# Binary cross-entropy on one core: runs of 8320 columns in place of 8192, the last four chunks 6272

## The chip, the cores and the metric

The kernel runs on one core of a Trainium2 chip, whose other cores are idle. The metric is device time in microseconds (us). Repeated runs of the kernel before spread over 1868.3 to 1873.6 us, so a difference under about 0.15% is not seen here.

## The reference

```python
def setup_inputs():
    return {
        "pred": np.random.uniform(0.01, 0.99, (8192, 8192)).astype(np.float32),
        "target": np.random.randint(0, 2, (8192, 8192)).astype(np.float32),
    }

def reference(pred, target):
    eps = 1e-7
    pred = np.clip(pred, eps, 1 - eps)
    return -(target * np.log(pred) + (1 - target) * np.log(1 - pred))
```

Two arrays of 268 MB are read and one is written. As target is 0 or 1, the kernel computes -ln|target - 1 + pred|.

## The kernel before

The arrays are taken as flat memory and cut into 64 chunks. A chunk is 128 rows of 8192 columns, one row for each of the 128 partitions of SBUF, the memory on the chip that the engines compute on. It lies in one piece in HBM, the large memory that holds the arrays, so the pitch (the distance from one partition's row to the next) is 32 KiB. Two rings of four slots in SBUF hold pred (fp32, computed on in place) and target (cast to bf16 by the load). In the profile's lines, DVE is VectorE and ACT is ScalarE, which compute, POOL is GpSimd, which issues most of the transfers, and SP (SPq) is SyncE, which issues the rest.

```python
W = 8192
SLOTS = 4
    # ...
    def chunks(ap):
        return ap.rearrange("r c -> (r c)").rearrange("(k p w) -> k p w", p=P, w=W)
    # ...
    def load(k):
        queue = nc.sync if k == 0 else nc.gpsimd
        queue.dma_start(out=slot(ring_p, k), in_=pred_c[k])
        nc.gpsimd.dma_start(out=slot(ring_t, k), in_=target_c[k])
    # ... store: as load, on nc.sync for the last two chunks
    # clip: one VectorE instruction on ring_p
    # front: VectorE (t - 1) + p, then ScalarE Abs and Ln; back: VectorE * -1
        for k in range(1, n - 1):
            clip(k)
            front(k)
            back(k - 1)
            store(k - 1)
            if k >= 2 and k - 2 + SLOTS < n:
                load(k - 2 + SLOTS)
    # ... the last chunk in four quarters of compute, stored in two halves
```

## Time and profile before

| | before |
|---|---|
| time, median of 3 runs | 1870.49 us |
| span of the profiled run | 1867.5 us |
| VectorE, ScalarE, POOL busy | 60%, 48%, 6% |
| HBM over the span | 431 GB/s |
| packets | 27,797 |

The page's slices cut the span in forty; a digit is the busy share in tenths. "Packets" are the single moves that the 16 DMA engines make. A load or a store of a chunk is 128 data packets of one row each; the 3088 packets under 512 B are 16 more for each of the 193 transfers, 4 B each in the records, and are called its completion writes here.

### The profile page before, as it was taken

What the parts mean: (1) busy time and instruction counts of PE and PEld (TensorE: products, weight loads), DVE (VectorE), ACT (ScalarE), POOL (GpSimd) and SP (SyncE); (2) the same over time, 40 slices, a digit from 0 to 9 for tenths busy, and PEclk for the clock granted to TensorE, in tenths of its full rate; (3) what the DMA queues carried; (4) which work ended last, traced back from release to release, by engine and by line L of the source; (5) the groups of instructions that cost most, each with busy time, mean ns of one, the idle gap of its engine ahead of it and who ended that gap; (6) DMA issues with size and microseconds to landing.
All of it is one profiled execution on the core that took longest, in us unless ns stands there. A gap on an engine that the chain in (4) does not pass through costs nothing.

```text
span 1867.5 us, 759 instructions
## 1 busy us (share of the span) xinstructions
DVE 1117.6 (60%) x199; ACT 902.4 (48%) x136; POOL 110.6 (6%) x193
## 2 busy tenths in 40 slices
DVE  4846564656656656566565665656656566566664
ACT  3643635546355364553644535445354463544635
POOL 0210000000000000000000000000000000000000
DMA  9999999999999999999999999999999999999999
GB/s 326 337 378 350 352 376 344 377 352 351 381 345 374 358 344 386 343 371 362 344 388 341 366 368 344 386 344 360 370 344 384 348 355 375 345 378 355 348 381 344
DMA packets 27797, 671.14 MB, mean 359 GB/s; under 512 B 3088, under 2 KB 3088, under 8 KB 3088
## 3 DMA queue, kind: packets, MB, share of 16 engines
q0 software_dynamic: 27216, 658.52, 98.9%
q1 hardware_dynamic: 576, 12.58, 1.6%
q14 instruction: 5, 0.04, 0.0%
HBM read 536.87 MB, written 268.44 MB: 431 GB/s over the span
## 4 chain that ended last, share of the span: by engine, by line
issue 87%; DMA 6%; POOL 5%; DVE 1%; ACT 1%; POOLq 0%; DVEq 0%; PEldq 0%
DMA ring_t<-in_target_dram 4%; DMA out_dram<-ring_p 2%; POOL ring_t L59 2%; POOL out_dram L63 2%; POOL ring_p L58 1%; DVE ring_p L73 1%; ACT ring_p L77 0%; ACT ring_p L76 0%; DVE ring_p L81 0%; POOLq L58 0%; DVEq L73 0%; PEldq L138 0%; POOLq L63 0%
## 5 line engine op out<-in xcount | busy, mean ns | idle before, releaser
L76 ACT ACTIVATE ring_p<-ring_p 128x8192 f32<-128x8192 f32 (+1 forms) x67 | 450.6, 6725 | 949.5 <-DVE ring_p L73 949.5
L73 DVE SCALAR_TENSOR_TENSOR ring_p<-ring_t,ring_p 128x8192 f32<-128x8192 bf16 (+1 forms) x67 | 556.6, 8309 | 326.0 <-DMA ring_t<-in_target_dram 326.0
L67 DVE TENSOR_SCALAR ring_p<-ring_p 128x8192 f32<-128x8192 f32 x64 | 283.3, 4426 | 406.6 <-DMA ring_p<-in_pred_dram 406.6
L77 ACT ACTIVATE ring_p<-ring_p 128x8192 f32<-128x8192 f32 (+1 forms) x67 | 450.6, 6725 | 2.1
L81 DVE TENSOR_SCALAR ring_p<-ring_p 128x8192 f32<-128x8192 f32 (+1 forms) x67 | 283.3, 4228 | 5.0 <-ACT ring_p L77 5.0
L63 POOL DMA_DIRECT2D out_dram<-ring_p x62 | 40.8, 659 | 1691.8 <-DVE ring_p L81 1661.8
L58 POOL DMA_DIRECT2D ring_p<-in_pred_dram x63 | 36.1, 574 | 18.7 <-DMA out_dram<-ring_p 18.4
L59 POOL DMA_DIRECT2D ring_t<-in_target_dram x64 | 35.3, 552 | 0.8 <-PEq L138 0.8
L87 ACT ACT_TABLE_LOAD x1 | 1.3, 1283 | 0.7 <-PEq L127 0.7
L86 DVE MEMSET warm<- 1x8 f32 x1 | 0.1, 65 | 0.8 <-PEq L127 0.8
L87 ACT ACTIVATE warm<-warm 1x8 f32<-1x8 f32 x1 | 0.2, 208 | 0.0
L127 POOL MEMSET const-float32-0.0<- 128x1 f32 x1 | 0.1, 98 | 0.2 <-issue 0.2
L127 POOL MEMSET const-bfloat16-1.0<- 128x1 bf16 x1 | 0.1, 101 | 0.0
L127 POOL MEMSET const-float32-1.0<- 128x1 f32 x1 | 0.1, 98 | 0.0
L127 POOL MEMSET const-uint8-127<- 128x1 uint8 x1 | 0.1, 98 | 0.0
## 6 DMA issues: line engine op xcount, KB each, us to landing
ring_p<-in_pred_dram POOLq DMA_DIRECT2D x63, 4096.0 KB, 34.5
out_dram<-ring_p POOLq DMA_DIRECT2D x62, 4096.0 KB, 25.3
ring_t<-in_target_dram POOLq DMA_DIRECT2D x64, 2048.0 KB, 43.7
ring_p<-in_pred_dram SPq DMA_DIRECT2D x1, 4096.0 KB, 19.5
out_dram<-ring_p SPq DMA_DIRECT2D x1, 4096.0 KB, 20.2
out_dram<-ring_p SPq DMA_DIRECT2D x2, 2048.0 KB, 11.6
```

Of the source, the lines that this page charges most:

```text
L58: queue.dma_start(out=slot(ring_p, k), in_=pred_c[k])
L59: nc.gpsimd.dma_start(out=slot(ring_t, k), in_=target_c[k])
L63: queue.dma_start(out=out_c[k, :, off : off + w], in_=slot(ring_p, k, off, w))
L67: nc.vector.tensor_scalar(out=p, in0=p, scalar1=EPS, scalar2=1 - EPS, op0=Alu.max, op1=Alu.min)
L73: nc.vector.scalar_tensor_tensor(out=p, in0=t, scalar=1.0, in1=p, op0=Alu.subtract, op1=Alu.add)
L76: nc.scalar.activation(out=p, in_=p, func=Act.Abs)
L77: nc.scalar.activation(out=p, in_=p, func=Act.Ln)
L81: nc.vector.tensor_scalar(out=p, in0=p, scalar1=-1.0, scalar2=None, op0=Alu.mult)
L86: nc.vector.memset(warm, 1.0)
L87: nc.scalar.activation(out=warm, in_=warm, func=Act.Ln)
L127: nc = _bacc.Bacc("TRN2", target_bir_lowering=False, num_devices=1)
```

## The change

The intent: at 8192 fp32 columns the partitions' rows start a power of two (32 KiB) apart. 8320 columns make it 33,280 B. Four narrower chunks take up the remainder and shorten the work after the last load.

```diff
-W = 8192
+UNIT = 128
+WIDE, LAST = 65 * UNIT, 49 * UNIT
 SLOTS = 4
+def plan(total):
+    n = (total - 4 * LAST) // WIDE
+    widths = [WIDE] * n + [LAST] * 4
+    assert sum(widths) == total
+    return widths
 ...
-    def chunks(ap):
-        return ap.rearrange("r c -> (r c)").rearrange("(k p w) -> k p w", p=P, w=W)
+    def chunk(ap, k):
+        flat = ap.rearrange("r c -> (r c)")
+        return flat[cols[k] * P : (cols[k] + widths[k]) * P].rearrange("(p w) -> p w", p=P)
 ...
-    ring_p = pool.tile([P, SLOTS * W], fp32, name="ring_p", tag="ring_p")
-    ring_t = pool.tile([P, SLOTS * W], bf16, name="ring_t", tag="ring_t")
+    ring_p = pool.tile([P, SLOTS * WIDE], fp32, name="ring_p", tag="ring_p")
+    ring_t = pool.tile([P, SLOTS * WIDE], bf16, name="ring_t", tag="ring_t")
 ...
-        q = W // 4
+        q = widths[n - 1] // 4
```

The rest of the diff gives each chunk its own width in load, store and compute.

More of the change, by code (lines that the diff above doesn't have):

```diff
@@ L38, with slot @@
     R, C = pred.shape
-    n = R * C // (P * W)
-    assert n * P * W == R * C and n > SLOTS
-    def chunks(ap):
-        return ap.rearrange("r c -> (r c)").rearrange("(k p w) -> k p w", p=P, w=W)
-    pred_c, target_c, out_c = chunks(pred), chunks(target), chunks(out)
+    widths = plan(R * C // P)
+    n = len(widths)
+    cols = [sum(widths[:k]) for k in range(n)]
+    def chunk(ap, k):
+        flat = ap.rearrange("r c -> (r c)")
+        return flat[cols[k] * P : (cols[k] + widths[k]) * P].rearrange("(p w) -> p w", p=P)
     pool = ctx.enter_context(tc.tile_pool(name="rings", bufs=1))
-    ring_p = pool.tile([P, SLOTS * W], fp32, name="ring_p", tag="ring_p")
-    ring_t = pool.tile([P, SLOTS * W], bf16, name="ring_t", tag="ring_t")
+    ring_p = pool.tile([P, SLOTS * WIDE], fp32, name="ring_p", tag="ring_p")
+    ring_t = pool.tile([P, SLOTS * WIDE], bf16, name="ring_t", tag="ring_t")
     warm = pool.tile([1, 8], fp32, name="warm", tag="warm")
-    def slot(ring, k, off=0, w=W):
-        c = k % SLOTS * W + off
+    def slot(ring, k, off=0, w=None):
+        w = w or widths[k]
+        c = k % SLOTS * WIDE + off
         return ring[:, c : c + w]
@@ L57, in load, with store, clip @@
         queue = nc.sync if k == 0 else nc.gpsimd
-        queue.dma_start(out=slot(ring_p, k), in_=pred_c[k])
-        nc.gpsimd.dma_start(out=slot(ring_t, k), in_=target_c[k])
-    def store(k, off=0, w=W):
+        queue.dma_start(out=slot(ring_p, k), in_=chunk(pred, k))
+        nc.gpsimd.dma_start(out=slot(ring_t, k), in_=chunk(target, k))
+    def store(k, off=0, w=None):
+        w = w or widths[k]
         queue = nc.sync if k >= n - 2 else nc.gpsimd
-        queue.dma_start(out=out_c[k, :, off : off + w], in_=slot(ring_p, k, off, w))
-    def clip(k, off=0, w=W):
+        queue.dma_start(out=chunk(out, k)[:, off : off + w], in_=slot(ring_p, k, off, w))
+    def clip(k, off=0, w=None):
         p = slot(ring_p, k, off, w)
@@ L69, in clip, with front @@
         )
-    def front(k, off=0, w=W):
+    def front(k, off=0, w=None):
         p, t = slot(ring_p, k, off, w), slot(ring_t, k, off, w)
@@ L77, in front, with back @@
         nc.scalar.activation(out=p, in_=p, func=Act.Ln)
-    def back(k, off=0, w=W):
+    def back(k, off=0, w=None):
         p = slot(ring_p, k, off, w)
```

## The prediction

> **What bounds the kernel now.** I read the page's span, its busy line and the slices first, then the DMA part, then the waits, then the timeline of a few chunks in the middle and of the end.
>
> ```profile
> span 1867.5 us, 759 instructions
> DVE 1117.6 (60%) x199; ACT 902.4 (48%) x136; POOL 110.6 (6%) x193
> ...
> DMA  9999999999999999999999999999999999999999
> ...
> DMA packets 27797, 671.14 MB, mean 359 GB/s; under 512 B 3088, under 2 KB 3088, under 8 KB 3088
> ...
> q0 software_dynamic: 27216, 658.52, 98.9%
> ...
> HBM read 536.87 MB, written 268.44 MB: 431 GB/s over the span
> ```
>
> No compute engine is over 60% busy, and the DMA engines are at nine tenths or more in all forty slices, the first and the last included. The 359 GB/s counts the bytes that a packet writes; a load of target reads fp32 and writes bf16, so it is counted at half. What the engines take in is the HBM line: 536.87 + 268.44 = 805.31 MB, 431 GB/s over the whole span. The kernel is one long stream of transfers with compute beside it.
>
> ```profile
> DVE ring_p L67 <- DMA ring_p<-in_pred_dram: 406.6, 61, 19.4
> DVE ring_p L73 <- DMA ring_t<-in_target_dram: 326.0, 63, 6.1
> ```
>
> In the waits (total us, times, longest) VectorE waits for loads 732.6 us in all; ScalarE waits for VectorE and is not what ends anything. The timeline of one chunk in the middle (start, us, engine and line) gives the period:
>
> ```profile
> 921.19 0.54 POOL L63 DMA_DIRECT2D out_dram<-ring_p  x1 [27.48 <-DVE ring_p L81]
> 921.72 0.54 POOL L58 DMA_DIRECT2D ring_p<-in_pred_dram  x1
> 922.24 0.55 POOL L59 DMA_DIRECT2D ring_t<-in_target_dram  x1
> ...
> 927.17 4.43 DVE L67 TENSOR_SCALAR ring_p<-ring_p 128x8192 f32<-128x8192 f32 x1 [6.27 <-DMA ring_p<-in_pred_dram]
> 936.93 8.69 DVE L73 SCALAR_TENSOR_TENSOR ring_p<-ring_t,ring_p 128x8192 f32<-128x8192 bf16 x1 [5.34 <-DMA ring_t<-in_target_dram]
> 945.54 4.42 DVE L81 TENSOR_SCALAR ring_p<-ring_p 128x8192 f32<-128x8192 f32 x1
> ```
>
> And the end:
>
> ```profile
> 1821.59 0.54 POOL L63 DMA_DIRECT2D out_dram<-ring_p  x1 [27.45 <-DVE ring_p L81]
> ...
> 1837.34 6.69 DVE L73 SCALAR_TENSOR_TENSOR ring_p<-ring_t,ring_p 128x2048 f32<-128x2048 bf16 x3 [0.97 <-DMA ring_t<-in_target_dram]
> ...
> 1854.77 1.23 DVE L81 TENSOR_SCALAR ring_p<-ring_p 128x2048 f32<-128x2048 f32 x1 [2.52 <-ACT ring_p L77]
> 1856.03 0.33 SPq L63 DMA_DIRECT2D out_dram<-ring_p  x1
> ```
>
> From the store issued at 921.19 to that at 1821.59 there are 31 chunks: 900.40 / 31 = 29.05 us a chunk. A chunk takes in 3 x 128 x 32,768 B = 12.58 MB: 433 GB/s. When POOL issues at 921.19, the loads queued before it still run until 927.17 and 936.93, so there are 15.7 us of work in the queue at each issue: the engines never run dry. The chain of waits calls 87% of the span "issue", because it follows POOL, which idles until its next turn; it names no cost.
>
> **What the Trainium skill says.** First, "DMA: Bandwidth & Descriptors", section "Where 436 GB/s comes from": 16 ports x 32 B x 850 MHz = 435.2 GB/s, 27.2 B/ns per engine. The trace agrees closely: the 433 GB/s of the steady chunks is 99.5% of it, and the trace's single packet records show 1213 ns as the median of a 32,768 B packet and 611 ns of the 16,384 B halves of the last store. The difference, 602 ns for 16,384 B, is 27.2 B/ns, which leaves about 9 ns fixed per packet. Consecutive packets overlap a little. Second, same page, section "Latency and other measured facts", the row on HBM row pitch at large powers of two: it measured 207 of 214 GB/s at a per-partition pitch of 512 KiB and half rate at 4 MiB, and nothing smaller. Here the pitch is 32 KiB and the packet medians stand at the port's rate, so this trace shows no such loss to recover. Third, same page, section "How a descriptor splits into AXI transactions": starts off a 256 B boundary cost beats. 33,280 B = 130 x 256, 25,088 = 98 x 256 and the half row of the last store 12,544 = 49 x 256, so all rows stay aligned; the trace of before can't show the unaligned case. Fourth, "SBUF — State Buffer", section "SBUF size: 192, 224, or 256?": about 208 KiB of a partition is usable. The rings grow from 4 x 8192 x 6 = 196,608 B to 4 x 8320 x 6 = 199,680 B, 195 KiB, and fit; no run shows the limit.
>
> **The change part by part.** The plan is 60 chunks of 8320 columns and four of 6272: 499,200 + 25,088 = 524,288 columns, 64 chunks as before. So nothing is removed or added: the same 759 instructions, the same 193 transfers of 128 rows, the same bytes, the same order and waits. Only sizes move.
>
> Transfers. One chunk is 24 packets per engine (3 x 128 / 16): 29.05 us / 24 = 1210.4 ns a packet, where the port's rate alone asks 32,768 / 27.2 = 1204.7. So 5.7 ns a packet are fixed, as an average with the overlap and the completion writes in it. A wide row: 33,280 / 27.2 + 5.7 = 1229.2 ns, x 24 = 29.50 us. A narrow row: 25,088 / 27.2 + 5.7 = 928.1 ns, x 24 = 22.27 us. Sum: 60 x 29.50 + 4 x 22.27 = 1770.0 + 89.1 = 1859.1 us against 64 x 29.05 = 1859.2. No change, and it doesn't matter whether the excess goes by packet or by byte.
>
> Compute, all beside the transfers. Wide: VectorE (4.43 + 8.69 + 4.42) x 65/64 = 17.8 us and ScalarE 2 x 7.03 x 65/64 = 14.3 us of a 29.50 us chunk. Narrow: x 49/64, 13.4 and 10.8 us of 22.27. The queue's reserve at each issue goes from 15.7 to 15.9 us, and to 12.0 us in the narrow chunks. The engines stay fed.
>
> The end. Before, the last load is waited for at 1837.34 and three stores, 12.58 MB or 29.05 us of transfer, are still to be moved; that puts the end of data near 1866. The last half store is issued 18.7 us after that load; its own data takes 29.05 / 6 = 4.8 us, so it had to be there by 29.05 - 4.8 = 24.2: 5.5 us of reserve. After, the stores left are 22.27 us, the last half 3.7 us, the deadline 18.6, and the chain of quarters shrinks to 18.7 x 49/64 = 14.3: 4.3 us of reserve. The end is bound by transfers in both, so the shorter last chunk buys nothing: the bytes that it no longer moves were moved earlier, at the same rate. What the narrow chunks do is leave the compute chain shorter beneath a queue that is shorter too.
>
> Start: the queue is filled by four loads at once and the first store comes long before they are done. A wider first chunk delays VectorE by about 0.3 us and the transfers by nothing.
>
> Sum: 1870.49 - 0.1, call it 1870.
>
> **The rivals.** (a) The pitch of 32 KiB does cost something and the new one frees it. For it speaks only the intent; against it, 99.5% of the port's rate. Were all 5.7 ns a packet to vanish, 64 x 24 x 5.7 ns = 8.8 us, giving 1862, 0.5% faster. A gain over 2% would need 37 us, four times that, and a rate of 440 GB/s, above the 435.2. (b) Rows over 32,768 B are cut into two packets. The largest packet in this trace is exactly 32,768 B, so it can't say. Then 60 x 24 = 1440 more packets per engine at 5.7 ns are +8.2 us, 1879; at 13 ns (the casting loads' packets have a larger fixed part: median 1227 ns for 32 KiB read) +19 us, 1889. Still about 1%. (c) The end is a compute chain after all, and shrinks: 4.4 us of quarters and 1.1 us of last store, 1865. The reserve of 5.5 us and the full last slice speak against it. (d) The new pitch hits the memory worse, or the engines drift apart more. Nothing speaks for it but that it is untried; to lose 2% each wide packet must take 26 ns more.
>
> **Range and chances.** Point 1870 us. The low end 1865 takes rival (c) or half of (a); the high end 1880 takes the mild form of (b). Faster by over 2% is shut out by the port's rate as the packets show it: 1%. Slower by over 2% needs (d) or a heavy form of (b): 3%. Within 2%: 96%.
>
> **What would show it.** In the profile of the changed kernel: 27,797 packets again (about 50,800 if wide rows are cut); stores of wide chunks issued 29.5 us apart and of narrow ones 22.3; the DMA row full to the last slice; HBM near 431 GB/s over the span; VectorE's three instructions at about 4.5, 8.83 and 4.5 us; a last issue some 14 us after the last load. Wrong would be: a wide period under 29.4 us (the pitch mattered), one over 29.6 (cut or slower packets), or DMA slices at the end below 9 (the narrow chunks let the queue run dry).

## The result

| | before | after |
|---|---|---|
| median of 4 runs | 1870.47 us | 1870.09 us |
| lowest to highest | 1869.30 to 1870.98 | 1869.18 to 1870.61 |
| span of the profiled run | 1867.5 us | 1867.3 us |
| packets | 27,797 | 27,797 |

The ratio is 0.9998, with a 95% interval of 0.9981 to 1.0016: the same.

From the page of the changed kernel:

```profile
span 1867.3 us, 767 instructions
DVE 1117.6 (60%) x199; ACT 902.3 (48%) x136; POOL 110.7 (6%) x193
...
DMA  9999999999999999999999999999999999999999
...
DMA packets 27797, 671.14 MB, mean 359 GB/s; under 512 B 3088, under 2 KB 3088, under 8 KB 3088
...
HBM read 536.87 MB, written 268.44 MB: 431 GB/s over the span
```

All that says what the time is made of is unchanged: DMA full in all forty slices, the same number of packets (so the rows over 32,768 B were not cut), 431 GB/s. The waits of VectorE (total us, times, longest):

```profile
DVE ring_p L78 <- DMA ring_p<-in_pred_dram: 410.1, 61, 20.0
DVE ring_p L84 <- DMA ring_t<-in_target_dram: 326.0, 63, 6.0
```

736.1 us in place of 732.6. The timeline in the middle, at the end of the wide chunks and at the last load and store (start, us, engine, line):

```profile
935.07 0.54 POOL L74 DMA_DIRECT2D out_dram<-ring_p  x1 [27.93 <-DVE ring_p L92]
...
951.07 8.83 DVE L84 SCALAR_TENSOR_TENSOR ring_p<-ring_t,ring_p 128x8320 f32<-128x8320 bf16 x1 [5.42 <-DMA ring_t<-in_target_dram]
959.81 4.49 DVE L92 TENSOR_SCALAR ring_p<-ring_p 128x8320 f32<-128x8320 f32 x1
...
1761.13 0.54 POOL L74 DMA_DIRECT2D out_dram<-ring_p  x1 [27.89 <-DVE ring_p L92]
1783.69 0.54 POOL L74 DMA_DIRECT2D out_dram<-ring_p  x1 [20.96 <-DVE ring_p L92]
1807.33 0.54 POOL L74 DMA_DIRECT2D out_dram<-ring_p  x1 [22.05 <-DVE ring_p L92]
1831.98 0.54 POOL L74 DMA_DIRECT2D out_dram<-ring_p  x1 [23.05 <-DVE ring_p L92]
...
1843.91 5.20 DVE L84 SCALAR_TENSOR_TENSOR ring_p<-ring_t,ring_p 128x1568 f32<-128x1568 bf16 x3 [0.70 <-DMA ring_t<-in_target_dram]
...
1858.65 0.33 SPq L74 DMA_DIRECT2D out_dram<-ring_p  x1
```

From 935.07 to 1761.13 are 28 wide chunks, 29.50 us each, where before it was 29.05; 65/64 of 29.05 is 29.50. The period grew by the bytes and by nothing else. The last three issues are 22.56, 23.64 and 24.65 us apart; that is taken up below.

The end, by stretches, before and then after (window, length, VectorE, ScalarE and POOL busy with counts, clock, DMA share, GB/s):

```profile
1855.00:1857.50 2.50, 1.00 (x1) 0.00 (x0) 0.00 (x0) 1.00 1.02 439
1857.50:1860.00 2.50, 0.00 (x0) 0.00 (x0) 0.00 (x0) 1.00 1.03 439
1860.00:1862.50 2.50, 0.00 (x0) 0.00 (x0) 0.00 (x0) 1.00 0.98 419
1862.50:1865.00 2.50, 0.00 (x0) 0.00 (x0) 0.00 (x0) 1.00 0.25 105
```

```profile
1855.00:1857.50 2.50, 0.69 (x1) 2.47 (x2) 0.00 (x0) 1.00 1.04 447
1857.50:1860.00 2.50, 0.98 (x1) 0.12 (x1) 0.00 (x0) 1.00 0.77 326
1860.00:1862.50 2.50, 0.00 (x0) 0.00 (x0) 0.00 (x0) 1.00 1.02 432
1862.50:1865.00 2.50, 0.00 (x0) 0.00 (x0) 0.00 (x0) 1.00 0.44 186
```

The share can exceed 1, as consecutive packets overlap. After, there is a dip to 0.77, about 0.25 x 2.5 = 0.6 us of missing transfer. The trace's packet records, counted by how many are in progress at a time, show what it is: at 1859.0 us six of the 16 engines have a packet and ten have none, while the last half store, issued at 1858.65, is still to come; from 1859.75 all 16 are busy. The kernel before has all 16 busy up to 1862.25. At 1863.0 there are still 16 busy after the change and 8 before it, but the last packet ends at 1865.8 us after and at 1866.0 before, and the span did not move.

### The profile page after: what moved, and what is told of

The parts are those of the page before. It is cut to its first block, busy times and chain, and to the rows that moved or that the text cites. A ratio compares the mean times of both kernels' runs of the same rounds, so it can differ in the third digit from the quotient of the medians.

```text
span 1867.3 us, 767 instructions
## 1 busy us (share of the span) xinstructions
DVE 1117.6 (60%) x199; ACT 902.3 (48%) x136; POOL 110.7 (6%) x193
## 2 busy tenths in 40 slices
DMA packets 27797, 671.14 MB, mean 359 GB/s; under 512 B 3088, under 2 KB 3088, under 8 KB 3088
## 4 chain that ended last, share of the span: by engine, by line
issue 88%; DMA 5%; POOL 5%; DVE 1%; ACT 1%; POOLq 0%; DVEq 0%; PEldq 0%
DMA ring_t<-in_target_dram 3%; DMA out_dram<-ring_p 2%; POOL ring_t L69 2%; POOL out_dram L74 2%; POOL ring_p L68 1%; DVE ring_p L84 1%; ACT ring_p L88 0%; ACT ring_p L87 0%; DVE ring_p L92 0%; POOLq L68 0%; DVEq L84 0%; PEldq L149 0%; POOLq L74 0%
## 5 line engine op out<-in xcount | busy, mean ns | idle before, releaser
L87 ACT ACTIVATE ring_p<-ring_p 128x8320 f32<-128x8320 f32 (+2 forms) x67 | 450.5, 6724 | 952.4 <-DVE ring_p L84 952.4
L84 DVE SCALAR_TENSOR_TENSOR ring_p<-ring_t,ring_p 128x8320 f32<-128x8320 bf16 (+2 forms) x67 | 556.6, 8310 | 326.1 <-DMA ring_t<-in_target_dram 326.0
L78 DVE TENSOR_SCALAR ring_p<-ring_p 128x8320 f32<-128x8320 f32 (+1 forms) x64 | 283.3, 4427 | 410.1 <-DMA ring_p<-in_pred_dram 410.1
L88 ACT ACTIVATE ring_p<-ring_p 128x8320 f32<-128x8320 f32 (+2 forms) x67 | 450.6, 6725 | 2.1
L92 DVE TENSOR_SCALAR ring_p<-ring_p 128x8320 f32<-128x8320 f32 (+2 forms) x67 | 283.3, 4229 | 4.0 <-ACT ring_p L88 4.0
```

What stands on the lines that cost most here:

```text
L78: nc.vector.tensor_scalar(out=p, in0=p, scalar1=EPS, scalar2=1 - EPS, op0=Alu.max, op1=Alu.min)
L84: nc.vector.scalar_tensor_tensor(out=p, in0=t, scalar=1.0, in1=p, op0=Alu.subtract, op1=Alu.add)
L87: nc.scalar.activation(out=p, in_=p, func=Act.Abs)
L88: nc.scalar.activation(out=p, in_=p, func=Act.Ln)
L92: nc.vector.tensor_scalar(out=p, in0=p, scalar1=-1.0, scalar2=None, op0=Alu.mult)
```

## The experiments

Two theories stood after the result. **One:** the kernel is a stream of transfers at the port's rate plus a few ns fixed per packet, the old pitch cost nothing, and the narrow end has nothing to shorten. **Two:** the pitch and the end each do something, and the two cancel. Twelve kernels were run on these and on what the pitch, the packet and compute cost. ("The port's rate" is the name that the prediction gives to 27.2 B/ns an engine. The packets show this rate; whether the port or something else sets it, no run separates.) In each, "before" is the kernel before on the same chip in the same rounds.

### The narrow end alone

```diff
-WIDE, LAST = 65 * UNIT, 49 * UNIT     # of the changed kernel
+WIDE, LAST = 64 * UNIT, 48 * UNIT     # 61 chunks of 8192, four of 6144
```

> The narrow end alone: 61 chunks of 8192 columns (pitch of 32 KiB kept) and four of 6144, 65 in all. Theory one, the stream of transfers is bound by the port's rate and a fixed few ns a packet: 61 x 29.05 + 4 x 24 x (24,576 / 27.2 + 5.7 ns) = 1772.1 + 87.3 = 1859.4 us of transfer against 1859.2, so 1870.6 us. Theory two, two effects cancelled in the change (the narrow end gains what the new pitch loses, or the reverse): 1866 or less, or 1874 or more.

Measured: 1869.59 us against 1870.09, ratio 0.9998 (0.9983 to 1.0013). As theory one has it. Its trace has the dip at the end too (seven engines with a packet at 1859.5 us).

### The wide runs alone

```diff
-WIDE, LAST = 65 * UNIT, 49 * UNIT     # of the changed kernel
+WIDE, LAST = 65 * UNIT, 8384
-    n = (total - 4 * LAST) // WIDE
-    widths = [WIDE] * n + [LAST] * 4
+    n = (total - 2 * LAST) // WIDE
+    widths = [WIDE] * n + [LAST] * 2  # 61 of 8320, two of 8384; slots of 8384
```

> The pitch alone, with no narrow end: 61 chunks of 8320 columns and two of 8384, 63 in all, no pitch a power of two. Theory one (port's rate): 61 x 29.50 + 2 x 24 x (33,536 / 27.2 + 5.7 ns) = 1799.5 + 59.5 = 1859.0, so 1870.3 us. Theory two (cancelling): the opposite sign of the run with the narrow end alone, 1874 or more or 1866 or less.

Measured: 1869.40 us against 1870.09, ratio 0.9995 (0.9980 to 1.0010). Its trace has no dip (all 16 engines busy up to 1862.0 us), so the dip is the narrow end's. Each part alone does nothing to the time; theory two falls. Neither half hides a gain or loss larger than 0.2%.

### Is the pitch ever a cost? 2 MiB, and a large pitch that is no power of two

```diff
-    .rearrange("(k p w) -> k p w", p=P, w=W)      # of the kernel before
+    .rearrange("(p k w) -> k p w", p=P, w=W)      # pitch 2 MiB
```

> The pitch made worse on purpose: each partition owns 524,288 columns in a row, so chunks of 8192 columns lie at a pitch of 2 MiB, a large power of two, with packets of the same 32 KiB. If the port's rate binds whatever the pitch: 1870 us. If the Trainium skill's row on large powers of two (164 of 214 GB/s at 2 MiB) carries over: packets of about 1.58 us and a period of 37.9 us, 64 x 37.9 + 11 = 2440 us.

Measured: 2059.31 us (2051.43 to 2066.52) against 1870.09, ratio 1.101 (1.0977 to 1.1043), result correct. So a power-of-two pitch can cost a great deal in this kernel, though a third of what the quoted row would have made of it. The page of this run:

```profile
span 2049.6 us, 759 instructions
...
DMA  9999999999999999999999999999999999999998
...
DMA packets 27797, 671.14 MB, mean 327 GB/s; under 512 B 3088, under 2 KB 3088, under 8 KB 3088
...
HBM read 536.87 MB, written 268.44 MB: 393 GB/s over the span
```

The engines are as "busy" as before, and move less: a full DMA row is no proof of full speed, and the HBM line (393 against 431 GB/s) must be read beside it.

The counterpart: a pitch nearly as large, 1,996,800 B.

```diff
-        return flat[cols[k] * P : (cols[k] + widths[k]) * P].rearrange("(p w) -> p w", p=P)
+        first = 0 if widths[k] == WIDE else n - 4      # of the changed kernel
+        wide = sum(x for x in widths if x == widths[k])
+        block = flat[cols[first] * P : (cols[first] + wide) * P].rearrange("(p w) -> p w", p=P)
+        c = cols[k] - cols[first]
+        return block[:, c : c + widths[k]]
```

> A large pitch that is no power of two: the 60 chunks of 8320 columns lie side by side in one block of pitch 1,996,800 B, the four of 6272 in one of 100,352 B. If only powers of two alias: 1870 us, and well below the run at 2 MiB if that is slow. If any pitch of megabytes costs: as slow as that run, 2400 us or so. If the port binds both: 1870 in both.

Measured: 1869.98 us, ratio 0.9999 (0.9982 to 1.0015). Megabytes of pitch cost nothing by themselves; 2 MiB does. (This run has the chunk widths of the changed kernel, the one at 2 MiB those of the kernel before; the widths alone make no difference, as the result shows.)

### Where the loss begins: 128 KiB, 512 KiB, 1 MiB

The edit is the same in all three, with g = 4, 16 or 32 chunks side by side:

```diff
-    .rearrange("(k p w) -> k p w", p=P, w=W)
+    .rearrange("(j p g w) -> j g p w", p=P, g=4, w=W)
-    in_=pred_c[k]               # target_c and out_c alike
+    in_=pred_c[k // 4, k % 4]
```

> The kernel before with four chunks side by side, so a pitch of 128 KiB, chunks of 8192 columns as before. If the loss seen at 2 MiB is one of very large powers of two: 1870 us. If it sets in just above 32 KiB, so that the kernel before stood at its edge: 1890 or more.

> The same with sixteen chunks side by side, a pitch of 512 KiB. The Trainium skill's row has 207 of 214 GB/s here; scaled by what 2 MiB lost in this case against that row (10% of the time against 30%), about 1%: 1890 us. No loss: 1870. The loss of 2 MiB already: 2050.

> The same with thirty-two chunks side by side, a pitch of 1 MiB, which the skill's row leaves out. Between the run at 512 KiB and that at 2 MiB: about 1960 us if the loss grows evenly; 1870 if it begins at 2 MiB.

| pitch | median us | ratio to before (95%) | packets of 32,768 B in the trace, 90th and 99th percentile, ns |
|---|---|---|---|
| 32 KiB (before) | 1870.49 | | 1213, 1226 |
| 128 KiB | 1870.08 | 0.9994 (0.9979 to 1.0009) | 1213, 1226 |
| 512 KiB | 1876.15 | 1.0027 (1.0011 to 1.0044) | 1213, 1258 |
| 1 MiB | 1910.13 | 1.0206 (1.0181 to 1.0231) | 1226, 1915 |
| 2 MiB | 2059.31 | 1.1010 (1.0977 to 1.1043) | 1580, 2419 |

Each ratio is to the kernel before in the same rounds (median 1870.36 us; 1870.09 for 2 MiB), not to the first row. The percentiles are of the POOL queue's packets; the median is 1213 ns in every row. The expectation at 512 KiB (1890) and that at 1 MiB (1960) were both too high: the loss grows steeply with each doubling rather than evenly. At 32 KiB the slow packets aren't there, and the kernel before does not stand at an edge: two doublings further there is still no loss. What makes a few packets slow no run shows.

### The fixed cost of a packet

```diff
-        queue.dma_start(out=slot(ring_p, k), in_=pred_c[k])
+        h = W // 4
+        for o in range(0, W, h):
+            queue.dma_start(out=slot(ring_p, k, o, h), in_=pred_c[k, :, o : o + h])
 # target's load and the store alike
```

> The kernel before with every transfer cut into column quarters, so four packets of 8 KiB a row in place of one of 32 KiB; bytes, chunks and waits of compute unchanged. Fixed cost by packet: 64 x 72 more packets an engine at 5.7 ns = +26 us, 1897; at the 9 ns that single packets show, +41 us, 1912. If the excess over the port's rate goes by bytes: 1870. If issuing on POOL (12 instead of 3 a chunk at 0.55 us) or completions set in: above 1930.

Measured: 1897.96 us (1897.49 to 1898.27) against 1870.01, ratio 1.0146 (1.0129 to 1.0163). 27.95 us over 64 x 72 = 4608 more packets an engine are 6.1 ns each, beside the 5.7 ns that the prediction took from one period and the port's rate. The ratio's interval is 24 to 30 us, 5.2 to 6.6 ns a packet, so the 5.7 ns fit and the 9 ns of single packets do not. The completion writes that came with the extra transfers are in this figure. In the page of this run:

```profile
DVE 1117.6 (59%) x199; ACT 902.3 (48%) x136; POOL 802.0 (42%) x760
...
DMA  9999999999999999999999999999999999999998
...
DMA packets 110604, 671.24 MB, mean 354 GB/s; under 512 B 12288, under 2 KB 12288, under 8 KB 45056
```

POOL's issuing rises from 6% to 42% of the span without emptying the queue: by the packet records an engine is without a packet for less than 3 us in all before the last stores end. So the 28 us are the packets'. The excess over the port's rate goes by packet and not by byte.

### Compute taken away

```diff
-        clip(0)
-            clip(k)
-        clip(n - 1)
```

> The kernel before without the clip, 64 VectorE instructions and 283 us of VectorE's 1118 (the result is the same for these inputs, which lie in 0.01 to 0.99). Theory one (transfers alone bind): 1870 us, VectorE near 45% busy and the 283 us back as waits for loads. If compute sets part of the period: 10 us faster or more, up to 64 x 4.4 = 283.

Measured: 1870.96 us against 1870.01, ratio 1.0002 (0.9987 to 1.0017), result correct. The page's busy line, and then the waits:

```profile
DVE 834.7 (45%) x135; ACT 902.2 (48%) x136; POOL 103.3 (6%) x193
```

```profile
DVE ring_p L73 <- DMA ring_t<-in_target_dram: 1008.4, 64, 25.7
```

VectorE's 283 us of clip turned into waits for the load: 1008.4 us in place of 732.6 in two groups, 276 more. A quarter of VectorE's work off the path is worth nothing.

### Bytes taken away

```diff
-        nc.gpsimd.dma_start(out=slot(ring_t, k), in_=target_c[k])
+        if k < SLOTS:
+            nc.gpsimd.dma_start(out=slot(ring_t, k), in_=target_c[k])
```

> A wrong result on purpose: target is loaded for the first four chunks only and these slots are read again, so 60 chunks move 16 packets an engine instead of 24, compute unchanged. If transfers alone bind: 4 x 29.05 + 60 x 19.37 = 1278 us, so about 1289 us in all (VectorE needs 17.5 of each 19.37). If compute or the waits between slots set a part of it: above 1310, with DMA slices below 9.

Measured: 1334.43 us (1332.32 to 1336.63), ratio 0.7132 (0.7119 to 0.7145), result wrong as intended. The direction is as expected and large, 536 us for 31% fewer bytes, but it is 45 us above the 1289 of transfers alone and beyond the 1310 named as the limit, so this run does not confirm pure transfer. The page of this run, and then its waits:

```profile
DVE 1117.7 (84%) x199; ACT 902.4 (68%) x136; POOL 82.2 (6%) x133
...
HBM read 285.21 MB, written 268.44 MB: 415 GB/s over the span
```

```profile
DVE ring_p L68 <- DMA ring_p<-in_pred_dram: 190.1, 61, 19.4
```

And its timeline:

```profile
714.55 0.53 POOL L64 DMA_DIRECT2D out_dram<-ring_p  x1 [19.00 <-DVE ring_p L82]
715.08 0.53 POOL L58 DMA_DIRECT2D ring_p<-in_pred_dram  x1
716.65 4.43 DVE L68 TENSOR_SCALAR ring_p<-ring_p 128x8192 f32<-128x8192 f32 x1 [2.39 <-DMA ring_p<-in_pred_dram]
...
734.43 0.53 POOL L64 DMA_DIRECT2D out_dram<-ring_p  x1 [18.82 <-DVE ring_p L82]
```

The period is 19.9 us, not 19.37. VectorE takes 17.5 of it and waits for the load the remaining 2.4. When POOL issues at 714.55, the load queued before it lands at 716.65: 2.1 us of reserve, where the kernel before has 15.7. A stretch at 605 to 610 us of the span shows a DMA share of 0.82 between neighbours above 1. The packets that do run are also slower on average (1252 ns against 1214 in the packet records of the POOL queue). Both have a part in the 45 us: the slower packets are 16,000 x 38 ns / 16 = 38 us of an engine's time, and an engine is without a packet for some 13 us (0.4 us in the kernel before). As consecutive packets overlap, these don't simply add, and why packets are slower here no run shows. For the kernel before and after it says one thing: removing bytes removes time at once, while removing compute removes none.

### The cast

```diff
-    ring_t = pool.tile([P, SLOTS * WIDE], bf16, name="ring_t", tag="ring_t")
+    ring_t = pool.tile([P, SLOTS * WIDE], fp32, name="ring_t", tag="ring_t")
-WIDE, LAST = 65 * UNIT, 49 * UNIT     # of the changed kernel
+WIDE, LAST = 50 * UNIT, 46 * UNIT     # 81 chunks of 6400, one of 5888
```

> Target kept as fp32, so no transfer casts: 81 chunks of 6400 columns and one of 5888 (four slots of 8 bytes a column leave no more). Against the next run, which has the same chunks with the cast: if the casting packets' longer duration (about 14 ns more each in the records) is time of the stream, 82 x 8 x 14 ns = 9 us faster, 1864; if it lies under the neighbouring packets, no difference, 1873.

And the same chunks with target in bf16 (only the second part of the edit):

> The chunks of the run without casts (81 of 6400 columns, one of 5888), target cast to bf16 as before. Theory one: same bytes, 18 x 24 = 432 more packets an engine at 5.7 ns = +2.5 us, 1873; at 9 ns +3.9 us, 1874. If the size of the chunk matters otherwise (reserve of the queue), more than 1880.

Measured: 1872.73 us without the cast (ratio 1.0011, 0.9996 to 1.0026) and 1871.15 with it (1.0003, 0.9988 to 1.0018). The gain of 9 us that the longer packets would allow isn't there; the sign is even the other way: each of the four runs without the cast (1872.18 to 1873.18) is slower than each of the four with it (1870.79 to 1871.79). That is 0.08%, less than the spread of the kernel before, and what makes it was not sought. The records of these two runs have casting packets of 964 ns at the median for 25,600 B read, and plain ones of 949, so the 14 ns or so add nothing to the stream; that they lie under the neighbouring packets, as the expectation has it, is the reading that fits, and was not seen directly. The +2.5 us expected for 18 more chunks is within what these rounds can't resolve.

No run points to a faster kernel. If the 5.7 ns of every packet vanished, 8.8 us or 0.5% would be gone; packets twice as long, if they stay whole, would give half of that, and two slots of them would fill the memory that four slots fill now. That was not built.

## Why the prediction was right

The time, 1870.09 us for 1870, came out as predicted. By its steps:

- **The bound.** Right. Taking compute away changed nothing (1870.96 us); taking bytes away changed 29%.
- **Wide chunks, 29.50 us.** Right: 29.50.
- **Fixed cost by packet, 5.7 ns.** Right in kind and size: 6.1 ns from quarter packets.
- **The pitch.** Right that no loss stood at 32 KiB, shown by the wide runs alone, by 128 KiB, and by the absence of slow packets. The doubt that it was untried is settled by a scale that runs from no loss to 10%.
- **Rows over 32,768 B cut in two.** Not so: 27,797 packets.
- **The end.** Right that transfers set it and that it gains nothing (the narrow end alone: 0.9998). The last load was waited for at 1843.91 and the last issue came at 1858.65, 14.7 us later for "some 14". But "the engines stay fed" was wrong, and so was the reserve of 4.3 us: ten of the 16 engines ran dry before the last half store came. The working took the 16 engines as one that ends near 1866. That is where the slowest ends: in the kernel before, 12 engines have a packet at 1862.5, 8 at 1863.0, 2 at 1865.0 and none at 1866.0, so the first ones had some 3.5 us less reserve than the 5.5 us worked out. The narrow end took away more of it. It cost no time because the slowest engines still had work: at no moment do fewer than six have a packet, and six are still moving data at 1863.5, when the other ten are done. (That these are the same six is inferred from the counts; the records name no engine.) So the unchanged end is not owed to the reserve that was worked out. The sign named for a queue that runs dry, DMA slices below 9, could not show it, as a slice is 46.7 us long.
- **Narrow chunks issued 22.3 us apart.** Wrong: 22.56, 23.64 and 24.65. The working gave a narrow chunk three narrow transfers. In the queue, a narrow chunk's two loads follow the store of a chunk three earlier, which is still wide: 29.50 / 3 + 2 x 22.27 / 3 = 24.68 us. The arrivals of target as VectorE sees them, 1747.61, 1772.30, 1797.01, 1821.65 and 1843.91, are 24.69, 24.71, 24.64 and 22.26 apart: three with a wide store between and the last with a narrow one. (The issues are not quite so far apart, as the compute between arrival and issue shrinks at the same time.) The sum is the same, as the narrow stores come at the end.
- **The same 759 instructions.** Wrong: 767. The work is the same (199, 136 and 193 on the three engines); the trace has four more semaphore instructions on VectorE and four on ScalarE. They show no cost.

## What to carry to other kernels

Before a layout is padded against powers of two, look whether there is anything to win: divide the bytes by the steady period, compare with the port's rate, and see whether the packets' upper percentiles lie above their median. Where the stream was at 99.5% of the rate, as here, pitch, tail and compute all lay beneath it, and only fewer bytes gave a gain; fewer packets should give up to 0.5% more, by estimate from the 5.7 ns. A full DMA row alone does not tell: in the run at 2 MiB it was as full at 393 GB/s as here at 431, and at the end of the changed kernel it hid ten idle engines.

## What the Trainium skill lacked or had wrong

- "DMA: Bandwidth & Descriptors", section "Latency and other measured facts", row on HBM row pitch: it begins at 512 KiB. These runs add that a pitch of 32 KiB or 128 KiB costs nothing (0.9994 at 128 KiB), 1 MiB 2.1% and 1,996,800 B nothing. Where both have a figure, this stream of loads and stores between HBM and SBUF lost less than the row's copies of 16 KiB rows between HBM tensors: 0.3% at 512 KiB for the row's 3% and 10% at 2 MiB for the row's 30% (214 over 207 and over 164).
- The same page, section "Measured (HBM→SBUF, 128 partitions, SWDGE, issued from GpSimd)", has about 10.5 ns a packet. That is the busy span of one whole transfer of 4 KB divided by its 64 packets, so it can't be set beside these runs' figure, which the page lacks: in a full queue of packets of 8 to 32 KiB, a further packet costs its engine 6.1 ns. A fixed overhead per packet stands on the page in cycles, for small descriptors; in ns, at these sizes, no page has it.
- No page has what a casting load costs in time: its packets are about 14 ns longer in the records (1227 for 1213), and no time of the stream (1871.15 with the cast, 1872.73 without).
